# A list schedule gets a new cost of a matmul, a longer step on one engine, and a port shared by VectorE and GpSimd

## The chip, the cores and the metric

The kernel runs on one core of one Trainium2 chip. The metric is the device time of one execution in microseconds (us), lower is better. Engines are named as in the profile: PE is TensorE (matmuls), PEld its weight loads, DVE is VectorE, ACT is ScalarE, POOL is GpSimd, and SP issues the DMAs.

## The reference

A decoder trunk of two layers over 256 tokens of 2048 features, all float32. Layer 0 mixes the tokens by an RWKV-7 recurrence, layer 1 by a gated DeltaNet; behind each stands a gated MLP whose up projection goes through a causal convolution of width 3. After each of the four sub-layers the sum with the residual is normalised. Cut to what matters:

```python
for i in range(2):
    mix = rwkv7_time_mix(x, ...) if i == 0 else gated_deltanet(x, ...)
    x = layer_norm(ALPHA * x + mix, ...)
    h = causal_dwconv(x @ w_up, conv_w) + conv_b          # 2048 -> 2 * 5504
    gate, up = split(h)
    x = layer_norm(ALPHA * x + (silu(gate) * up) @ w_down, ...)
```

The weights are some 500 MB of float32 that are read once. The two recurrences are computed in chunks of 128 tokens; each chunk needs the inverse of a triangular matrix per head.

## The kernel before

**Products.** A float32 product is made of three f32r ones: each operand is split into hi and lo. `weights` (line 633 on) loads a weight tile `raw` of 128x1024, rounds it to `whi` on ACT, and takes `wlo = raw - whi` by `two`. A block of a projection is then a matmul of `whi` with hi and lo of the tokens side by side (512 columns) and one of `wlo` with hi alone (256 columns). The projections with tokens on the partitions (`proj_tm`, tile `tm`) use 512 columns throughout.

**Stages.** First the RWKV layer: token mixing and projections (`mixhl`), then eight units of the recurrence (`rwkv_unit`, four heads each, up to four units at a time) beside further projections; then the MLP (`ffn`: up projection, convolution on DVE in tile `acc`, `hhl` as its split result, down projection); then the DeltaNet's input projection with its convolution (tile `acc` again) beside eight more units (`gdn_unit`, up to two at a time) and its output projection; then the second MLP and the output.

**The order of the work is made by a planner.** The kernel doesn't issue instructions as they are written. `Plan.record` (line 305) takes each down with its estimated cost from `cost` (line 578), and with the instructions that it depends on. Consecutive matmuls into one tile are one step of at most 700 ns. There is one main stream (the projections) and one side stream per unit of a recurrence. `order` (line 366) is a list schedule: it keeps for each engine the time at which it is free, and again and again issues the candidate with the earliest start. On PE a side stream goes ahead of the main one at the same start; on the other engines the older unit goes first and the main stream last. A step is ready when what it depends on has ended, plus a latency: `LAT` and `LAT_TO` between engines, nothing from PE to PE, and `LAT_SAME` = 60 ns on one and the same other engine. The order found is static: every engine then runs its own list in turn and waits by semaphores, and the DMAs that SP issues stand in that order too.

**The choice of the engine is the planner's.** `two` (line 302) takes down an element-wise operation of two tensors with two forms, on DVE and on POOL, and `copy` one on ACT and on DVE. The candidate of a form sorts by its start plus what the form costs above the cheaper one, so the engine that ends first gets it. Estimated are, for n elements of a partition, n / 0.96 + 68 ns on DVE (1135 at 1024, 601 at 512, 335 at 256) and 2.1 n + 150 on POOL (2300, 1225, 688). The start of such a step may lie before steps that are already issued on other engines, since its place in the sorting is later than its start.

**What is not in the plan.** Each engine's steps are taken to last their estimate whatever the others do. Of the matmul, `cost` says max(107, n / 2.4 + 3) ns at full clock (216 at 512 columns, 110 at 256), doubled for float32 operands; the plan also models PE's clock, full or half, by how busy PE was.

Of the kernel before, what the change touches and what calls it, by code (L numbers as in the profile page):

```python
# [12 lines left out]
F32 = mybir.dt.float32  # L13
F32R = mybir.dt.float32r
U32 = mybir.dt.uint32
AF = mybir.ActivationFunctionType
ALU = mybir.AluOpType
AX = mybir.AxisListType

P = 128  # L20
T = 256
D = 2048
KB = D // P
# [8 lines left out]
# columns of the parameter array  # L32
# [9 lines left out]
# columns of the constant array  # L42
# [8 lines left out]
def constants():  # L51
# [10 lines left out]
    # inside a block of 32 the blocks of 8; inside a block of 8 the diagonal  # L62
    parts["blk8"] = i[:, None] // 8 % 4 == i[None, :32] // 8
    parts["eye8"] = i[:, None] % 8 == i[None, :8]
    # -1 where row and column lie in the same block of 32 but the row's block of 8 comes after the column's;
    # rows and columns in the order of digits (block of 8 in its block of 32, block of 32, place in 8)
    parts["neg32"] = -parts["blk32"][:, :96]
    o = digits()
# [10 lines left out]
def digits():  # L79
    """The tokens of a chunk ordered by block of 8 in its block of 32, then by block of 32."""  # L80
    return np.arange(P).reshape(-1, 4, 8).transpose(1, 0, 2).ravel()


class Buf:
    """A tile of a pool; it comes to be when the first instruction that touches it is issued."""
# [39 lines left out]
def arranged(x, pat, kw):  # L125
    """rearrange for numpy."""
# [27 lines left out]
class View:  # L154
    """A part of a Buf, as the instructions take it."""
# [25 lines left out]
    def region(self):  # L181
        """What it covers: the partitions and the elements of a partition, as bits. A bank of PSUM goes as one."""
# [53 lines left out]
class Op:  # L236
    __slots__ = ("lazy", "eng", "calls", "dur", "preds", "succ", "soft", "at", "bufs", "news", "stream", "idx", "npred", "ready",
                 "out", "fn", "alts", "least", "held", "evac", "table")
# [15 lines left out]
class Plan:  # L254
    """Takes instructions down in the order of the program, then issues them in an order in which the engines,
    each of which runs its instructions in turn, wait little for each other: a list schedule by estimated costs.
    The hazards between them fix what may change places; Tile draws the waits for the order issued."""
# [10 lines left out]
    # ---------------------------------------------------------------- taking down  # L268
# [7 lines left out]
    def op(self, eng, stream):  # L276
# [3 lines left out]
        o.npred, o.held, o.evac, o.lazy, o.table = 0, 0.0, [], self.lazy, None  # L280
        stream.ops.append(o)
# [11 lines left out]
    def either(self, *forms):  # L293
        """Forms (engine, function, arguments, keywords) of one instruction: the engine that ends first gets it."""
        o = self.record(*forms[0], also=[v for f in forms[1:] for v in parts(*f[2:])[1]])
        o.alts = {eng: (fn, a, kw, cost(eng, fn, a, kw, parts(a, kw)[1])) for eng, fn, a, kw in forms}
        o.least = min(x[3] for x in o.alts.values())

# [6 lines left out]
    def record(self, eng, fn, args, kw, also=()):  # L305
# [11 lines left out]
        o.dur += dur  # L317
        if fn == "activation":
            o.table = TABLES.get(args[2])
# [1532 lines left out]
```

## Time and profile before

| | |
|---|---|
| median of 3 runs | 3161.74 us (3155.25 to 3171.25) |
| the profiled execution, from its first to its last instruction | 3153.7 us |
| PE busy in it | 3008.4 us (95%) |
| DVE busy | 2374.1 us (75%) |
| ACT busy | 1688.0 us (54%) |
| POOL busy | 748.4 us (24%) |
| mean granted clock of PE | 0.982 of full |
| HBM read | 498 MB, 159 GB/s over the span |

No time is given of the profiled execution beside its span. Busy time is the union of an engine's instructions; PE's ends are modelled, so that a PE shown as 100% busy still says nothing about the pace of its matmuls, which follows from their number in a stretch. Every instruction is recorded by one helper (line 558), so groups are told apart by the names of their tiles: `wlo<-raw,whi` is the instruction that writes `wlo` from `raw` and `whi`.

### The profile page before, as it was taken

The numbers are of one execution on the slowest core, as the hardware profiler recorded it, in microseconds if no ns is written. First come the engines' busy times: TensorE is split into PE (matmuls) and PEld (weight loads), VectorE is DVE, ScalarE is ACT, GpSimd is POOL, SyncE is SP. The second block draws the span as 40 slices with busy tenths as digits, with TensorE's granted clock in tenths as the row PEclk, the third lists the DMA queues.
The fourth block names the chain that finished last, engine by engine and source line by source line (L and its number), as shares of the span: only waits on it lengthen the run. The fifth ranks groups of instructions, "written<-read, shape, count | busy, mean of one in ns | idle before, by whom it ended". The sixth has DMA issues, their size and how long they took to land.

```text
span 3153.7 us, 47051 instructions
## 1 busy us (share of the span) xinstructions
PE 3008.4 (95%) x17379; PEld 2569.3 (81%) x17379; DVE 2374.1 (75%) x3817; ACT 1688.0 (54%) x2895; POOL 748.4 (24%) x666
## 2 busy tenths in 40 slices
PE   8898988899999999999899999999999999999998
PEld 6786777788888888888788888888788888888886
DVE  6878888877877776446989989889777877777445
ACT  4555555545555555334555555556556555555333
POOL 2524345523310100002322221223133401010001
PEclk9998999999999999999999999999999999999999
DMA  6453112125666665554645555454455666565555
GB/s 207 149 164 105 62 53 77 67 94 177 193 188 188 188 188 189 191 187 157 191 136 145 154 153 148 134 147 142 146 179 171 204 190 187 187 187 184 194 189 188
DMA packets 436230, 503.19 MB, mean 160 GB/s; under 512 B 22784, under 2 KB 367264, under 8 KB 436000
## 3 DMA queue, kind: packets, MB, share of 16 engines
q1 hardware_dynamic: 436000, 500.19, 50.3%
q8 instruction: 136, 2.23, 0.3%
q14 instruction: 94, 0.77, 0.1%
HBM read 498.00 MB, written 2.13 MB: 159 GB/s over the span
## 4 chain that ended last, share of the span: by engine, by line
PE 74%; DVE 16%; issue 4%; ACT 3%; POOL 2%; DMA 1%; SPq 0%; DVEq 0%; ACTq 0%; POOLq 0%
PE mm L558 44%; PE tm L558 22%; DVE wlo L558 4%; DVE acc L558 2%; DVE mixt L558 1%; PE y L558 1%; ACT whi L558 1%; PE gm L558 1%; PE au L558 1%; DVE y L558 1%; PE n L558 1%; DVE c L558 1%; DVE uc L558 1%; PE kv L558 1%; DVE glo L558 0%
## 5 line engine op out<-in xcount | busy, mean ns | idle before, releaser
L558 PE MATMUL mm<-xhl,whi 128*128 128x512 f32 (+1 forms) x4376 | 1525.4, 395 | 4.4 <-POOL xhl L558 2.2
L558 DVE TENSOR_TENSOR wlo<-raw,whi 128x1024 fp32r<-128x1024 f32 (+2 forms) x894 | 1105.3, 1238 | 538.1 <-ACT whi L558 535.5
L558 ACT CAST whi<-raw 128x1024 fp32r<-128x1024 f32 (+3 forms) x929 | 949.4, 1023 | 748.6 <-PE tm L558 291.9
L558 PE MATMUL mm<-xhl,wlo 128*128 128x256 f32 (+1 forms) x4376 | 1209.4, 281 | 12.2 <-DVE wlo L558 11.4
L558 PEld LDWEIGHTS mm<-xhl,whi 128*128 128x128 f32 x4376 | 816.6, 189 | 177.8 <-POOL xhl L558 3.3
L558 PEld LDWEIGHTS mm<-xhl,wlo 128*128 128x128 f32 x4376 | 825.7, 189 | 29.9 <-DVE wlo L558 15.3
L558 PE MATMUL tm<-whi,hhl 128*128 128x512 f32 x1312 | 408.1, 392 | 0.0
L558 PE MATMUL mm<-mixhl,whi 128*128 128x512 f32 (+1 forms) x832 | 313.7, 414 | 13.4 <-DVE mixhl L558 8.1
L558 DVE SCALAR_TENSOR_TENSOR acc<-pre,taps,acc 128x256 f32<-128x256 f32 x536 | 312.1, 590 | 7.1 <-ACT acc L558 0.3
L558 PEld LDWEIGHTS tm<-whi,hhl 128*128 128x128 f32 x1312 | 246.4, 188 | 54.7
L558 POOL TENSOR_TENSOR hhl<-acc,hhl 128x256 fp32r<-128x256 f32 x86 | 96.4, 1121 | 814.3 <-ACT hhl L558 814.3
L558 PE MATMUL mm<-mixhl,wlo 128*128 128x256 f32 (+1 forms) x832 | 245.1, 300 | 16.3 <-DVE wlo L558 13.6
L558 PE MATMUL tm<-wlo,hhl 128*128 128x512 f32 x656 | 256.7, 391 | 0.7 <-DVE wlo L558 0.6
L558 ACT COPY addp<-mm 128x256 f32<-128x256 f32 x321 | 118.0, 368 | 175.1 <-PE mm L558 174.8
L558 PEld LDWEIGHTS mm<-mixhl,whi 128*128 128x128 f32 (+1 forms) x832 | 162.3, 197 | 50.6 <-DVE mixhl L558 8.4
L558 PEld LDWEIGHTS mm<-mixhl,wlo 128*128 128x128 f32 (+1 forms) x832 | 164.1, 197 | 28.5 <-DVE wlo L558 18.7
L558 POOL TENSOR_TENSOR wlo<-raw,whi 128x1024 fp32r<-128x1024 f32 (+3 forms) x35 | 72.6, 2078 | 406.4 <-ACT whi L558 395.1
L558 PE MATMUL tm<-whi,ohl 128*128 128x512 f32 x480 | 156.6, 398 | 0.2 <-DVE zt L558 0.2
L558 ACT ACTIVATE acc<-pre,taps 128x256 f32<-128x256 f32 x236 | 135.7, 575 | 24.0 <-DVE pre L558 23.5
L558 PEld LDWEIGHTS tm<-wlo,hhl 128*128 128x128 f32 x656 | 123.2, 188 | 27.6 <-DVE wlo L558 1.5
L558 DVE TENSOR_TENSOR pre<-mm,addp 128x256 f32<-128x256 f32 x236 | 99.0, 419 | 56.8 <-ACT addp L558 56.2
L558 POOL TENSOR_TENSOR mixhl<-mixt,mixhl 128x256 fp32r<-128x256 f32 x71 | 78.4, 1125 | 138.5 <-ACT mixhl L558 138.5
(346 smaller groups left out, 3644.0 us busy)
## 6 DMA issues: line engine op xcount, KB each, us to landing
raw<-in_ffn_w_up SPq DMA_DIRECT2D x336, 512.0 KB, 3.6
raw<-in_gdn_w_in SPq DMA_DIRECT2D x192, 512.0 KB, 3.8
raw<-in_ffn_w_down SPq DMA_DIRECT2D x168, 512.0 KB, 3.6
raw<-in_gdn_w_out SPq DMA_DIRECT2D x64, 512.0 KB, 3.6
raw<-in_rw_w_v SPq DMA_DIRECT2D x32, 512.0 KB, 3.3
raw<-in_rw_w_r SPq DMA_DIRECT2D x32, 512.0 KB, 3.3
raw<-in_rw_w_o SPq DMA_DIRECT2D x32, 512.0 KB, 3.6
raw<-in_rw_w_k SPq DMA_DIRECT2D x31, 512.0 KB, 4.4
```

The source lines that it names most:

```text
L558: i = getattr(getattr(self.real, o.eng), fn)(*(val(a) for a in args), **{k: val(a) for k, a in kw.items()})
```

## The change

Nothing that is computed changes, and no instruction is added or removed; the planner's model changes, and with it the order of the steps and which of DVE, POOL and ACT gets a step with several forms. The cost of a matmul becomes max(111, n / 2.4 + 3 + 16 n / 512) ns (232 at 512 columns, 118 at 256; the floor of float32 ones 2 x 111). `LAT_SAME` becomes 115. And steps of DVE and POOL may be marked as users of a shared port; one that would start within the last marked step of the other engine starts at that one's end.

```diff
     def either(self, *forms):
+        o.port = {eng: ported(eng, fn, a, parts(a, kw)[1]) for eng, fn, a, kw in forms}
     def record(...):
+        o.port[eng] = ported(eng, fn, args, rds)
     def order(self):
+        port = {e: (0.0, 0.0) for e in PORT}
...
                         if b.read is not None and b.read[0] != e:
                             r = max(r, b.read[1] + LAT[b.read[0]] + LAT_TO[e])
+                    if e in PORT and o.port[e]:
+                        t0, t1 = port[PORT[e]]
+                        if t0 <= max(f, r) < t1:
+                            r = t1
                     s = max(f, r)
                     if o.alts:
                         s += o.alts[e][3] - o.least
...
             t = s + dur
+            if e in PORT and o.port[e]:
+                port[e] = s, t
+PORT = {"vector": "gpsimd", "gpsimd": "vector"}
+def ported(eng, fn, args, rds):
+    if eng == "gpsimd":
+        return bool(rds)
+    if eng != "vector":
+        return False
+    wide = [v for v in rds if math.prod(v.shape[1:]) > 1 and not (v.buf.pool is not None and v.buf.pool.psum)]
+    out = args[0].buf.pool
+    return len(wide) > 1 or bool(wide) and fn in ("tensor_copy", "tensor_scalar") and not (out is not None and out.psum)
 def cost(eng, fn, args, kw, rds):
-            return 2 * max(107.0 * out.shape[0] / P, n / 1.2 + 3)
-        return max(60.0 if fn == "transpose" and args[1].dtype == F32R else 107.0 * out.shape[0] / P, n / 2.4 + 3)
+            return 2 * max(111.0 * out.shape[0] / P, n / 1.2 + 3)
+        return max(111.0 * out.shape[0] / P, n / 2.4 + 3 + 16 * n / 512)
-LAT_SAME = 60.0
+LAT_SAME = 115.0
```

So marked are: on POOL whatever reads a tensor; on DVE an operation with two or more tensors from SBUF, and a copy or `tensor_scalar` from SBUF to SBUF. The rest of the diff takes comments out.

## Rows read from the trace of the kernel before

**Rows 1.** Busy time by stretch; columns as in the first line.

```profile
core 0: us, PE busy (x) PEld busy (x) DVE busy (x) ACT busy (x) POOL busy (x), PEclk, DMA share, GB/s
0.00:900.00 900.00, 816.07 (x5144) 695.03 (x5145) 717.05 (x1239) 483.32 (x962) 354.63 (x352) 0.95 0.39 125
230.00:690.00 460.00, 407.07 (x2909) 348.25 (x2908) 383.58 (x777) 248.70 (x570) 212.02 (x220) 0.92 0.22 74
1000.00:1100.00 100.00, 100.00 (x572) 87.12 (x571) 72.08 (x100) 58.18 (x90) 11.20 (x10) 1.00 0.61 188
1400.00:2500.00 1100.00, 1050.97 (x6265) 901.25 (x6264) 924.33 (x1647) 614.95 (x1098) 295.45 (x233) 0.99 0.52 157
1500.00:2300.00 800.00, 759.49 (x4782) 655.93 (x4780) 704.09 (x1318) 447.08 (x805) 186.69 (x131) 0.99 0.51 150
2500.00:3154.00 654.00, 641.51 (x3342) 546.18 (x3341) 415.01 (x525) 328.61 (x466) 59.16 (x48) 0.99 0.58 189
```

**Rows 2.** PE's waits over the whole span: us in total, times, longest.

```profile
PE mm L558 <- DVE wlo L558: 25.0, 20, 3.3
PE blocks L558 <- DVE spread L558: 16.6, 9, 4.3
PE gm L558 <- DVE glo L558: 9.6, 4, 4.4
```

**Rows 3.** Timeline from 405 to 420 us: start, us, engine, instruction, [idle before].

```profile
409.45 5.66 POOL L558 TENSOR_TENSOR wlo<-raw,whi 128x1024 fp32r<-128x1024 f32 x2
...
410.04 2.87 DVE L558 TENSOR_TENSOR ld<-lt,cst 128x512 fp32r<-128x512 f32 x1
412.83 2.35 DVE L558 TENSOR_TENSOR t<-blocks,v 128x56 f32<-128x56 f32 x1
...
416.71 0.68 DVE L558 TENSOR_TENSOR glo<-AR,ghi 128x512 fp32r<-128x512 f32 x1
...
417.44 0.58 PE L558 MATMUL gm<-glo,ghi 64*128 64x256 f32 x2 [4.42 <-DVE glo L558]
...
417.86 0.41 DVE L558 TENSOR_TENSOR_SCAN c<-one,sw_u 128x128 f32<-128x128 f32 x1
```

**Rows 4.** DVE's groups by shape, 1500 to 2300 us: busy us, mean ns | idle before.

```profile
L558 DVE TENSOR_TENSOR wlo<-raw,whi 128x1024 fp32r<-128x1024 f32 x210 | 265.4, 1264 | 37.8 <-ACT whi L558 35.9 <-ACT th L558 0.2
L558 DVE SCALAR_TENSOR_TENSOR acc<-pre,taps,acc 128x256 f32<-128x256 f32 x192 | 113.4, 611 | 1.1 <-ACT acc L558 0.3
...
L558 DVE SCALAR_TENSOR_TENSOR z_u<-th,zt 128x256 f32<-128x256 f32 x32 | 20.3, 635 | 0.3 <-ACT th L558 0.2
...
L558 DVE SCALAR_TENSOR_TENSOR v_u<-th,acc 128x256 f32<-128x256 f32 x32 | 13.2, 417 | 0.1
```

**Rows 5.** DVE's groups by shape, 900 to 1300 us (up projection).

```profile
L558 DVE TENSOR_TENSOR wlo<-raw,whi 128x1024 fp32r<-128x1024 f32 x137 | 167.8, 1225 | 102.8 <-ACT whi L558 102.8
L558 DVE SCALAR_TENSOR_TENSOR acc<-pre,taps,acc 128x256 f32<-128x256 f32 x124 | 66.3, 535 | 2.1
```

**Rows 6.** DVE's groups by shape, 230 to 690 us (RWKV units).

```profile
L558 DVE TENSOR_TENSOR wlo<-raw,whi 128x1024 fp32r<-128x1024 f32 x39 | 51.3, 1318 | 10.3 <-ACT whi L558 10.2
L558 DVE TENSOR_TENSOR_SCAN c<-one,sw_u 128x128 f32<-128x128 f32 x32 | 20.5, 672 | 0.0
```

**Rows 7.** Timeline of DVE from 1003 us: two dependent steps, then the next.

```profile
1003.86 0.99 DVE L558 SCALAR_TENSOR_TENSOR acc<-pre,taps,acc 128x256 f32<-128x256 f32 x2
1004.89 0.42 DVE L558 TENSOR_TENSOR acc<-acc,gs 128x256 f32<-128x256 f32 x1
```

**Rows 8.** PE's main matmuls of 512 columns, 1500 to 2300 us.

```profile
L558 PE MATMUL mm<-xhl,whi 128*128 128x512 f32 x1504 | 537.1, 398 | 0.0
```

**Rows 9.** POOL's groups by shape: `hhl` over the span, `ld` and `y` in 1500 to 2300 us.

```profile
L558 POOL TENSOR_TENSOR hhl<-acc,hhl 128x256 fp32r<-128x256 f32 x86 | 96.4, 1121 | 814.3 <-ACT hhl L558 814.3
...
L558 POOL TENSOR_TENSOR ld<-lt,cst 128x512 fp32r<-128x512 f32 x16 | 24.4, 1544 | 0.0
...
L558 POOL TENSOR_TENSOR y<-z,cst 128x512 fp32r<-128x512 f32 x15 | 21.0, 1404 | 88.7 <-ACT z L558 68.3 <-DVE z L558 20.2
```

More of the change, by code (lines that the diff above doesn't have):

```diff
@@ L237 @@
     __slots__ = ("lazy", "eng", "calls", "dur", "preds", "succ", "soft", "at", "bufs", "news", "stream", "idx", "npred", "ready",
-                 "out", "fn", "alts", "least", "held", "evac", "table")
+                 "out", "fn", "alts", "least", "held", "evac", "table", "port")
 class Stream:
@@ L280, in op @@
         o.npred, o.held, o.evac, o.lazy, o.table = 0, 0.0, [], self.lazy, None
+        o.port = {}
         stream.ops.append(o)
```

## The prediction, made before the changed kernel was run

> **What bounds the kernel now.** I first read the busy time by stretch. In the up projection every microsecond of PE is taken, at full clock [rows 1]; there a stretch of 100 us holds 572 matmuls, 286 pairs of 512 and 256 columns, so a pair takes 349.7 ns. No order of the steps can make these stretches shorter. What an order can win is PE's idle time elsewhere: 900 - 816.07 = 83.9 us up to 900 us, 1100 - 1050.97 = 49.0 us from 1400 to 2500 us, and 12.5 us in the last stretch. Inside these lie the two stages of the recurrences, with 52.9 us idle of 460 (230 to 690 us) and 40.5 of 800 (1500 to 2300 us); DVE is busy for 83% and 88% of them, so it has 76.4 and 95.9 us idle [rows 1]. In the first of them the granted clock is 0.92, in the second 0.99.
>
> The second view is that of PE's waits: the longest totals are all ended by DVE (`wlo` 25.0 us, `spread` 16.6, `glo` 9.6) [rows 2]. So PE is the bound, and where it stalls it stalls for a DVE that is behind its plan.
>
> The third view says why it is behind. In the timeline POOL runs two `wlo` from 409.45 us for 5.66 us; the DVE steps `ld` and `t` that overlap them take 2.87 and 2.35 us, while `glo`, as large as `ld`, takes 0.68 us when POOL is quiet, and PE waits 4.42 us for DVE [rows 3]. The reader is to see that two engines which share nothing in the old plan hold each other up.
>
> **The change part by part.** No instruction comes or goes; the plan's order and the choice between DVE, POOL and ACT do. I price four parts.
>
> *The port.* What the collisions take from DVE has no row of its own, so I bound it by groups of one shape. From 1500 to 2300 us: 210 `wlo` at 1264 ns against 1225 in the up projection lose 8.2 us; 192 `acc` at 611 against 535 lose 14.6; 32 `z_u` at 635 against 417 of `v_u`, of the same shape, lose 7.0 [rows 4, 5]. That is 29.8 of the 399 us that these groups are busy, 7.5%, or 53 us of DVE's 704. From 230 to 690 us: 39 `wlo` at 1318 lose 3.6 us of 51.3 (7%), and 32 scans `c` at 672 against 410 in the timeline lose 8.4 of 20.5 (41%) [rows 3, 5, 6]; the two together lose 17%, or 64 of DVE's 384 us, with 27 and 157 as ends. In sum some 117 us of locked DVE time in the two stages.
>
> How much of it will the new test avoid? It moves a start only if that falls inside the other engine's *last* marked step. Two kinds are shown. `hhl` becomes ready in the middle of a DVE `wlo`, and POOL took all 86 at 1121 ns each [rows 9]; that kind is caught, since POOL must now wait for the same instant at which DVE is free. The two `wlo` on POOL [rows 3] were put there because DVE had a backlog; such a step is planned with a start that lies before DVE's last step, so the test passes it by, though DVE's next marked steps then wait for it in the plan as well. Between nothing and all I take half, one kind of the two: 58 us. Of that the end sees what PE no longer waits for: at least PE's share of the two engines' idle time, 93 / (93 + 172) = 0.35, at most all of it. I take a half, near the low end because DVE has idle time to absorb the rest: **-29 us**.
>
> *Steps that go from POOL to DVE.* In the up projection DVE is 72% busy beside a full PE, so 86 `hhl` at some 0.42 us cost nothing; were DVE full there, they would cost 36 us. In the DeltaNet units the 31 `ld` and `y` [rows 9] would bring DVE at most 31 x 0.68 = 21 us, against 96 us idle, and come out 0.8 us earlier each, 25 us in all on chains. I set the two against each other: **0**, ends -25 and +21.
>
> *The longer step on one engine.* Two dependent `acc` and the start of the next step stand 515 ns apart (1004.89 - 1003.86, halved) [rows 7]; the plan's cost of one is 396, so the real gap is 119 ns, which 115 meets and 60 does not. In 1500 to 2300 us the 192 `acc` make at most 128 such gaps, 15 us of DVE that other steps can now be planned into; by the same share of 0.35, less what was filled anyway: **-3 us**, ends -15 and 0.
>
> *The pace of the matmuls.* The row gives 349.7 ns a pair [rows 1]; the old cost is 326, the new one 350. So the plan had PE 24 ns a pair too fast, and with 1504 pairs [rows 8] PE came to its places in the DeltaNet stage up to 36 us later than planned. That error was a cushion: DVE could be late without PE waiting. It goes. If half the port (26 us) and the gaps (15 us) are now planned instead, 41 us of planned lateness stand in for 36 us of cushion, and little is lost; I put **+3 us**, ends 0 and +36.
>
> The Trainium skill, "TensorE: Matmul & The Clock Gate", section "Back-to-back issue gap", speaks against this part: it gives N / 2.4 + 2.5 ns from matmul to matmul, 325 ns a pair, by which the old cost was right and the new one too slow. By it the new plan would place side work where PE stands 36 us too early, and the sum would be some 30 us higher, no gain at all. The measured 349.7 ns decides against the page here, so the sum goes by the row and this way gets no chance of its own.
>
> SP's loads move with the steps that free their buffers. The DMA share is 0.22 to 0.61 in these stretches [rows 1] and no wait of PE's above is ended by a DMA, so I price that at nothing; a load on the path would cost PE what it waits for it.
>
> The sum: -29 + 0 - 3 + 3 = -29 us on the profiled execution, 3153.7 - 29 = 3124.7. That execution lies 8.0 us under the median of the runs, so I forecast 3124.7 + 8.0 = **3133 us**, 0.9% less.
>
> **The rivals.** *The chains stay (within 0.5%).* DVE loses less to the port, but what it wins is its own idle time: a unit's next step still waits for a matmul, and PE stalls at the same places for the same chains. For it: DVE has 172 us idle in the two stages while PE waits for it. Against: in rows 3 the wait is the collision itself. Priced with a tenth avoided, seen by PE at the low end: 117 x 0.1 x 0.35 = 4 us, so 3158, and 16 us either way of the median counts as the same.
>
> *The cushion is missed (slower).* Place: the DeltaNet stage, where 1504 pairs stand beside an 88% busy DVE. Mechanism: side matmuls are now put into PE's fixed list 24 ns a pair earlier, while backlogged POOL steps escape the test, so DVE is as late as before and PE waits for it. Price: 36 us less the 15 us of gaps now planned, +21, so 3183 us. It decides if under a third or so of the locked time is avoided. For it: the escape is in the code. Against: most of what collides in rows 4 is an in-order neighbour of a `wlo`, the kind the test sees.
>
> *The change does not bite.* The test passes nearly all by and the greedy order comes out much as before: 3162 us, within the run-to-run spread of 3155 to 3171. For it: DVE is saturated enough for starts in the past to be common. Against: two costs change beside it, and every tie after the first is drawn anew.
>
> **How the numbers follow.** A measurement of this kernel tells about 0.5%, 16 us, from no change. Forecast 0.46 (faster), chains 0.26 and no bite 0.06 (within), cushion 0.22 (slower). The low end is three quarters of the locked time avoided and three quarters of that seen by PE, 117 x 0.56 = 66 us: 3095. The high end is the cushion's 3183 and a little for the runs: 3185. A lower bound than this would need the clock as well: 0.92 over 460 us leaves up to 37 us in the RWKV stage if PE, less often idle, were granted full clock throughout, which I do not count. The forecast's own range is 3095 to 3146.
>
> **What would show it.** Right: the group `hhl` moves largely to DVE; `acc` and `z_u` from 1500 to 2300 us come down towards 535 and 417 ns; PE's waits on `wlo`, `spread` and `glo` shrink; PE's idle time in the two stages falls from 93 us to some 65; 100 us of up projection still hold 572 matmuls. Wrong: the DVE groups get shorter and PE's idle time doesn't (chains); PE's idle time from 1500 us on rises past 60 us with waits ended by DVE (cushion); POOL keeps its groups and their mean times (no bite). A change of the time in the MLP stretches would contradict all of it.

## The result, and the profile after

The changed kernel takes **3217.11 us** (median of 4 runs, 3203.66 to 3220.57); the kernel before, run beside it, 3163.12 us (4 runs, 3155.25 to 3171.25). The ratio is **1.0143, 95% interval 1.0113 to 1.0173**: slower by 1.4%, where 0.9% less was forecast, and outside the range.

The profiled executions have spans of 3153.7 us (before) and 3202.0 us (after). I cut both at the same marks of the program: the first product of an RWKV unit, the first product of the first MLP's up projection, its down projection, the DeltaNet projections, the DeltaNet output projection, and the second MLP. The first view is the busy time by stretch. For the kernel before, its RWKV units with the projections that run beside them, then the MLP's up projection:

```profile
core 0: us, PE busy (x) PEld busy (x) DVE busy (x) ACT busy (x) POOL busy (x), PEclk, DMA share, GB/s
250.40:742.30 491.90, 440.94 (x3060) 376.05 (x3059) 405.21 (x812) 261.18 (x583) 218.71 (x226) 0.93 0.24 79
742.30:1236.70 494.40, 489.06 (x2817) 425.92 (x2816) 364.61 (x507) 288.29 (x459) 82.94 (x74) 1.00 0.61 186
1475.10:2209.50 734.40, 692.52 (x4443) 601.80 (x4442) 656.56 (x1255) 416.77 (x768) 190.12 (x136) 0.99 0.52 149
2209.50:2411.60 202.10, 199.63 (x981) 164.46 (x979) 150.74 (x230) 112.61 (x196) 55.61 (x53) 0.99 0.47 165
```

The last two lines are its DeltaNet units and the DeltaNet output projection. The same stretches of the changed kernel follow, with 100 us of its up projection and the 800 us that answer to the last stretch but one of [rows 1]:

```profile
247.50:777.20 529.70, 473.83 (x3060) 406.18 (x3059) 411.01 (x796) 262.50 (x591) 232.72 (x234) 0.85 0.22 73
777.20:1276.10 498.90, 491.90 (x2818) 428.75 (x2817) 357.42 (x531) 289.38 (x460) 73.15 (x50) 0.99 0.60 184
...
1000.00:1100.00 100.00, 100.00 (x572) 87.07 (x571) 69.57 (x103) 57.91 (x90) 9.76 (x5) 1.00 0.60 188
...
1514.80:2254.20 739.40, 696.52 (x4467) 605.93 (x4466) 648.68 (x1252) 420.34 (x775) 179.25 (x127) 0.98 0.51 147
2254.20:2455.00 200.80, 195.16 (x957) 160.51 (x955) 157.63 (x258) 111.13 (x192) 36.81 (x35) 1.00 0.48 168
...
1540.00:2340.00 800.00, 753.83 (x4752) 651.31 (x4750) 695.84 (x1324) 442.93 (x794) 186.50 (x124) 0.98 0.50 148
```

37.8 of the 48.3 us that the span grew lie in the RWKV stage, and it isn't waiting that grew there. PE's idle time in it is 491.9 - 440.94 = 51.0 us before and 529.7 - 473.83 = 55.9 us after. What grew is its *busy* time: as many matmuls, 3060, take 32.9 us longer, and the granted clock is 0.85 where it was 0.93. By (1 - clock) x length, what TensorE lacks to its full clock in this stage went from 34 us to 79. Over the whole span, with the clocks that the two profiles show (0.982 and 0.965), it went from 57 to 112, 55 us more in a span that is 48.3 longer. The up projections give 4.5 us (494.4 to 498.9) and about as much in the second MLP; the DeltaNet units 5 (734.4 to 739.4), in which PE is idle for 42.9 us where it was 41.9.

Where the clock is lost, a finer cut of the changed kernel shows, and under it the same view for the projections' matmuls alone (those that read `mixhl`; the output projection's, which read `yhl`, begin later, at 569 us before and at 607 us after):

```profile
500.00:520.00 20.00, 18.88 (x145) 16.52 (x144) 14.65 (x27) 11.15 (x28) 13.79 (x17) 1.00 0.08 27
520.00:540.00 20.00, 8.51 (x38) 6.29 (x38) 18.34 (x43) 8.74 (x22) 10.16 (x12) 0.58 0.12 40
540.00:560.00 20.00, 19.75 (x122) 17.04 (x120) 8.68 (x18) 9.72 (x27) 1.97 (x5) 0.50 0.00 1
560.00:580.00 20.00, 20.00 (x87) 18.52 (x88) 7.06 (x22) 4.25 (x12) 7.37 (x8) 0.50 0.17 53
580.00:600.00 20.00, 19.19 (x120) 17.36 (x119) 17.12 (x37) 8.13 (x17) 7.88 (x7) 0.71 0.37 111
...
520.00:560.00 40.00, 0.84 (x2) 0.55 (x2) 0.00 (x0) 0.00 (x0) 0.00 (x0) 0.54 0.06 20
560.00:600.00 40.00, 13.11 (x45) 9.27 (x46) 0.00 (x0) 0.00 (x0) 0.00 (x0) 0.61 0.27 82
```

From 520 us PE is busy for 8.51 us of 20, and the granted clock falls from 1.00 to 0.50, which is 1.2 GHz. Then PE is busy all the time, and the clock stays at 0.50 for 40 us more: what it works on are the units' small products, beside 2 matmuls of the projections from 520 to 560 us. It rises as the projections come back. In the kernel before, 520 to 560 us hold 62 of them at a clock of 0.88:

```profile
480.00:520.00 40.00, 12.58 (x52) 9.15 (x53) 0.00 (x0) 0.00 (x0) 0.00 (x0) 0.93 0.16 53
520.00:560.00 40.00, 17.67 (x62) 11.78 (x61) 0.00 (x0) 0.00 (x0) 0.00 (x0) 0.88 0.33 113
```

What the half clock costs one instruction shows in PE's groups by shape, first in 541 to 579 us, then in 600 to 638 us of the changed kernel (busy us, mean ns):

```profile
L569 PE MATMUL au<-u,lt 128*128 128x64 f32 x16 | 3.8, 417 | 0.0
L569 PE MATMUL mm<-mixhl,whi 128*128 128x512 f32 x5 | 3.3, 657 | 0.0
...
L569 PE MATMUL mm<-mixhl,whi 128*128 128x512 f32 x10 | 3.6, 393 | 0.0
L569 PE MATMUL au<-u,lt 128*128 128x64 f32 x16 | 2.1, 276 | 0.0
```

Then what the change was to do. The groups that answer to [rows 4] (DVE, 1540 to 2340 us), [rows 6] (DVE, 247.5 to 777.2 us) and [rows 9] (POOL):

```profile
L569 DVE TENSOR_TENSOR wlo<-raw,whi 128x1024 fp32r<-128x1024 f32 x210 | 274.3, 1306 | 33.5 <-ACT whi L569 32.4
L569 DVE SCALAR_TENSOR_TENSOR acc<-pre,taps,acc 128x256 f32<-128x256 f32 x188 | 100.9, 564 | 2.4 <-ACT acc L569 1.7
L569 DVE SCALAR_TENSOR_TENSOR z_u<-th,zt 128x256 f32<-128x256 f32 x32 | 16.7, 531 | 0.0
...
L569 DVE TENSOR_TENSOR wlo<-raw,whi 128x1024 fp32r<-128x1024 f32 x42 | 52.5, 1251 | 14.9 <-ACT whi L569 13.8 <-PE lora L569 0.8
L569 DVE TENSOR_TENSOR_SCAN c<-one,sw_u 128x128 f32<-128x128 f32 x32 | 17.4, 563 | 0.0
...
L569 POOL TENSOR_TENSOR hhl<-acc,hhl 128x256 fp32r<-128x256 f32 x42 | 79.9, 1903 | 806.1 <-ACT hhl L569 806.1
```

Half of the `hhl` left POOL, and the rest take 1903 ns instead of 1121. `acc`, `z_u` and `c` came down a part of the way (611 to 564, 635 to 531, 672 to 563), but `wlo` went up in 1540 to 2340 us, from 1264 to 1306. DVE's busy time there fell by 8 us (704.09 to 695.84), and in the RWKV stage it rose by 6 with 16 steps fewer. PE's waits that answer to [rows 2], over the whole span:

```profile
PE blocks L569 <- DVE spread L569: 26.9, 8, 8.1
PE mm L569 <- DVE wlo L569: 24.8, 17, 3.3
PE mm L569 <- DVE mixhl L569: 9.8, 2, 9.6
...
PE gm L569 <- DVE glo L569: 3.9, 2, 3.2
```

`wlo` is as it was, `spread` is longer by 10 us, and the waits for `glo` fell from 9.6 us to 3.9; the wait of 8.1 us is the one at 520 us, just ahead of the stretch at half clock.

### The profile page after: what moved, and what is told of

It reads as the page before. It is cut to its first block, busy times and chain, and to the rows that moved or that the text cites. A ratio compares the mean times of both kernels' runs of the same rounds, so it can differ in the third digit from the quotient of the medians.

```text
span 3202.0 us, 47006 instructions
## 1 busy us (share of the span) xinstructions
PE 3044.8 (95%) x17379; PEld 2604.6 (81%) x17379; DVE 2374.7 (74%) x3884; ACT 1692.9 (53%) x2906; POOL 695.0 (22%) x588
## 4 chain that ended last, share of the span: by engine, by line
PE 68%; DVE 9%; issue 3%; ACT 2%; POOL 2%; DMA 1%; DVEq 0%; POOLq 0%; ACTq 0%
PE mm L569 39%; PE tm L569 22%; DVE wlo L569 3%; DVE acc L569 1%; PE y L569 1%; ACT whi L569 1%; PE au L569 1%; PE n L569 1%; PE gm L569 0%; PE kv L569 0%; DVE uc L569 0%; PE yT L569 0%; PE o L569 0%; PE u L569 0%; PE du L569 0%
## 5 line engine op out<-in xcount | busy, mean ns | idle before, releaser
L569 DVE TENSOR_TENSOR wlo<-raw,whi 128x1024 fp32r<-128x1024 f32 (+1 forms) x900 | 1109.1, 1234 | 546.4 <-ACT whi L569 543.4
L569 DVE SCALAR_TENSOR_TENSOR acc<-pre,taps,acc 128x256 f32<-128x256 f32 x536 | 277.4, 541 | 6.7 <-ACT acc L569 1.7
L569 POOL TENSOR_TENSOR hhl<-acc,hhl 128x256 fp32r<-128x256 f32 x42 | 79.9, 1903 | 806.1 <-ACT hhl L569 806.1
L569 POOL TENSOR_TENSOR wt<-raw,wt 128x512 fp32r<-128x512 f32 x9 | 12.7, 1413 | 451.5 <-ACT wt L569 451.5
L569 PEld LDWEIGHTS tm<-whi,ohl 128*128 128x128 f32 x480 | 90.2, 188 | 21.2 <-DVE zt L569 1.8
```

Of the source, the lines that this page charges most:

```text
L569: i = getattr(getattr(self.real, o.eng), fn)(*(val(a) for a in args), **{k: val(a) for k, a in kw.items()})
```

## The experiments

The theories that the runs were to tell apart: **the port rule** (P in the expectations) spoils the RWKV stage; **the cushion** (C) of the old matmul cost is missed (the rival of the prediction); **scatter** (S), a greedy schedule whose order any edit of its costs redraws; and **starved projections** (H), in which the order leaves a stretch of the RWKV stage to the units' products, and TensorE falls to half clock. Ratios are to the kernel before, run beside each (medians of 3163 to 3170 us). "The loss" is (1 - granted clock) x length of the RWKV stage, with the clock as the view prints it, to two places.

### The parts, one at a time

The kernel before with the new matmul cost alone:

```
-            return 2 * max(107.0 * out.shape[0] / P, n / 1.2 + 3)
-        return max(60.0 if fn == "transpose" and args[1].dtype == F32R else 107.0 * out.shape[0] / P, n / 2.4 + 3)
+            return 2 * max(111.0 * out.shape[0] / P, n / 1.2 + 3)
+        return max(111.0 * out.shape[0] / P, n / 2.4 + 3 + 16 * n / 512)
```

> Only the matmul cost is the new one (111 and 16 n / 512); the port is not looked at and LAT_SAME is 60. Theory P (the port part spoils the RWKV stage): the time stays within 10 us of before, PE's first matmul of the first MLP (mm<-xhl) starts at 742 us give or take 8, and no stretch at half clock is longer than 15 us. Theory C (the lost cushion of 24 ns a pair): 15 to 40 us over before, with PE's idle time from 1500 to 2300 us (40.5 before) up by 10 us or more. Theory S (scatter: any other order of the greedy list lands somewhere else in the RWKV stage): the first mm<-xhl moves by 5 to 35 us either way, all of the time's difference lies before it, and the DeltaNet stage keeps its length within 6 us.

Measured 3220.2 us, ratio 1.0162 (1.0127 to 1.0197), over what any of the three forecast. Its DeltaNet units and their output projection:

```profile
1514.70:2264.30 749.60, 700.56 (x4467) 606.23 (x4466) 649.71 (x1264) 420.22 (x771) 175.38 (x120) 0.98 0.52 145
2264.30:2471.20 206.90, 198.61 (x955) 162.60 (x954) 152.05 (x239) 109.62 (x189) 62.05 (x56) 0.98 0.49 164
```

Its profiled execution has a span of 3213.8 us, 60.1 more than before. Of these 38.9 lie in the RWKV stage (491.9 to 530.8) and 20.0 in the two stretches shown, where PE is idle for 57.3 us instead of 44.4: so C's sign, idle time up by 10 us or more, is there too, at the smaller part of the loss. The kernel before with LAT_SAME alone:

```
-LAT_SAME = 60.0
+LAT_SAME = 115.0
```

> Only LAT_SAME is the new one (115). Theory P: within 10 us of before. Theory C: within 10 us of before, or a few us faster, as the cushion is kept and DVE's steps are planned better. Theory S: off by 5 to 35 us either way in the RWKV stage, the rest of the time unchanged within 8 us.

Measured 3156.98 us, 0.9961 (0.9942 to 0.9979): the only kernel of the study below the kernel before beyond its interval. Where the 13 us come from the profiles don't show: the execution profiled here took 3159.45 us, the one of the kernel before 3155.25. The port rule alone (`ported`, `port` and the test in the loop over candidates, with the old costs):

```
+                    if e in PORT and o.port[e]:
+                        t0, t1 = port[PORT[e]]
+                        if t0 <= max(f, r) < t1:
+                            r = t1
```

> Only the port is new; matmul cost and LAT_SAME are the old ones. Theory P: 30 to 50 us over before, the first mm<-xhl at 770 us or later, with a stretch at half clock of 30 us or more between 450 and 650 us. Theory C: 10 to 40 us faster than before, since the cushion is kept and DVE is locked less. Theory S: off by 5 to 35 us either way, all of it in the RWKV stage.

Measured 3183.14 us, 1.0045 (1.0024 to 1.0066): 13 us over before, not P's 30 to 50, and within the range of S. Then the changed kernel with one part taken out, first the matmul cost, then the port test:

```
-            return 2 * max(111.0 * out.shape[0] / P, n / 1.2 + 3)
-        return max(111.0 * out.shape[0] / P, n / 2.4 + 3 + 16 * n / 512)
+            return 2 * max(107.0 * out.shape[0] / P, n / 1.2 + 3)
+        return max(60.0 if fn == "transpose" and args[1].dtype == F32R else 107.0 * out.shape[0] / P, n / 2.4 + 3)
```

> The changed kernel with the old matmul cost: port and LAT_SAME 115 stay. Theory C (the new pace is what costs, by the lost cushion): at or under before, 3140 to 3165 us, with a DeltaNet stage of 725 us or less. Theory H (what costs is a stretch of the RWKV stage in which the main projections have next to nothing ready, so that PE falls to half clock): this order too has such a stretch, so the RWKV stage is 20 to 40 us longer than before's 491.8, with over 55 us lost to half clock in it, whatever the cost of a matmul; in all 3165 to 3195.

```
-                    if e in PORT and o.port[e]:
+                    if False and o.port[e]:
```

> The changed kernel without the port: the new pace and LAT_SAME 115. Theory C: slower still than the changed kernel, as the cushion is gone and nothing stands for it: 3215 us or more. Theory H: the RWKV stage is again some 450 us plus what half clock loses in it, 510 to 535 us, and the total 3190 to 3225.

Measured 3236.43 us, 1.0216 (1.0177 to 1.0255) without the matmul cost, and 3226.64 us, 1.0194 (1.015 to 1.0237) without the port rule. The first missed both its forecasts. Its RWKV stage is starved (553.2 us, a loss of 89), as H had it, and its DeltaNet units are short (703.8 us), as C had it, but the output projection behind them took 251.2 us instead of 202.1. The second came out as C forecast (3215 or more) and just over H's range. Taking either part out makes the changed kernel no faster. The port rule and LAT_SAME cost +0.45% and -0.4% alone and +2.2% together, so the parts have no prices that add up. The cushion doesn't explain the changed kernel: with the old matmul cost back it is the slowest of all, and PE's idle time in its DeltaNet units, where the cushion would be missed, rose by 1 us only. Nor is the port rule the one cause, since without it the kernel is as slow.

### An edit that means nothing

The kernel before with LAT_SAME moved by 2 ns, up and then down:

```
-LAT_SAME = 60.0
+LAT_SAME = 62.0
```

> The kernel before with LAT_SAME 62 in place of 60: a change of the model by 2 ns that means nothing. Theories P and C: within 6 us of before, since nothing of port or cushion changes. Theory S: 8 us or more off before, either way, in the RWKV stage, though the model is the same to 2 ns.

```
-LAT_SAME = 60.0
+LAT_SAME = 58.0
```

> The kernel before with LAT_SAME 58 instead of 60, an edit that says nothing of the hardware. Its order has a stretch poor in the projections' wide matmuls near the middle of the RWKV stage and one at its end. Starved projections: 3170-3190, loss by the clock in the stage over 45 us. Without that theory: as the kernel before, 3155-3175.

Measured 3186.89 us, 1.0065 (1.0043 to 1.0087) for 62, which S alone allowed, and **3215.3 us, 1.0157 (1.0131 to 1.0183)** for 58: an edit of 2 ns that tells the planner nothing new costs as much as the whole change. It missed what was expected on the upper side. Its RWKV stage and, in it, the projections' matmuls:

```profile
249.10:786.90 537.80, 478.89 (x3059) 411.72 (x3058) 406.76 (x815) 260.71 (x582) 212.16 (x224) 0.84 0.22 72
...
480.00:520.00 40.00, 15.29 (x64) 11.19 (x64) 0.00 (x0) 0.00 (x0) 0.00 (x0) 0.91 0.13 40
520.00:560.00 40.00, 0.00 (x0) 0.00 (x0) 0.00 (x0) 0.00 (x0) 0.00 (x0) 0.52 0.06 20
560.00:600.00 40.00, 14.45 (x64) 10.27 (x64) 0.00 (x0) 0.00 (x0) 0.00 (x0) 0.80 0.37 119
```

It is the changed kernel's picture: 40 us without one matmul of the projections, a clock of 0.52 there, 0.84 over the stage, and the same matmuls busy for 478.89 us instead of 440.94. A neighbour of the changed kernel:

```
-LAT_SAME = 115.0
+LAT_SAME = 117.0
```

> The changed kernel with LAT_SAME 117 instead of 115, an edit without meaning. Its order has the same poor stretch in the middle of the RWKV stage, and a milder one behind it. Starved projections: 3190-3212, loss 55-75 us. Scatter without a cause: 3160-3240. If it and another neighbour stay above 3190 the slowdown belongs to the new rules and not to one unlucky order.

Measured 3215.62 us, 1.0166 (1.0131 to 1.0201), with a stage of 535.4 us at 0.84: as slow as the changed kernel, and slower than expected. Here 2 ns moved the time by no more than the noise. By what was put on record, two neighbours over 3190 would lay the slowdown on the new rules; the kernel before at LAT_SAME 58, which has none of them and is as slow, speaks against that reading.

### One slot more for what starves

A projection's output waits in one of eight slots (`uin`) until its unit has used it; when all are held, no projection can end, and none of its matmuls can go beside the units. That is read from the code; no trace shows that the slots are what is missing at 520 us of the changed kernel. A ninth slot, paid for with one of the units' work slots, in the changed kernel and in the kernel before:

```
-DEPTH_R, NS2_R, NIN, NC8_R = 4, 27, 8, 5
+DEPTH_R, NS2_R, NIN, NC8_R = 4, 26, 9, 5
```

> The changed kernel with all three parts, and nine slots in place of eight for what the projections hand to a unit (NIN 9), paid by one working slot of the units (NS2_R 26 in place of 27). Theory H: the main projections can run ahead of the units again, the long stretch at half clock goes (none over 25 us), the RWKV stage comes back to 480 to 505 us, and the total to 3160 to 3185, though the model is the changed one. Theory C: the DeltaNet stage and the cushion are untouched, so at most 10 us come back: 3205 or more.

> The kernel before with the same edit as the first run with nine slots (NIN 9, NS2_R 26). Starved projections: the kernel before has no long starved stretch to cure and pays one work slot: 3160-3190. If a ninth slot is worth 20 us to any order: 3140-3150.

Measured 3196.46 us, 1.0094 (1.0059 to 1.0129) for the changed kernel, and 3193.98 us, 1.0094 (1.0061 to 1.0127) for the kernel before. The same edit takes 21 us off the one and puts 27 on the other, and both missed what H expected: the stages are 520.1 us (480 to 505 expected) and 538.0. The ninth slot paid for in other groups, in the changed kernel:

```
-DEPTH_R, NS2_R, NIN, NC8_R = 4, 27, 8, 5
+DEPTH_R, NS2_R, NIN, NC8_R = 4, 27, 9, 4
...
-NMORE, NLNT = 8, 4
+NMORE, NLNT = 8, 3
```

> The changed kernel with nine slots instead of eight for what the projections hand to the units, paid for in two other groups (NC8_R 4, NLNT 3) and not in the units' work slots as in the run with nine before. Starved projections: in this order the projections' wide matmuls stand evenly between the units' products through the whole stage, so the RWKV stage is at most 510 us, the loss by the granted clock there at most 50 us, and the time 3160-3185. Mere scatter of the greedy schedule: no preference, 3195-3235 as for the other orders under the new costs.

Measured 3191.74 us, 1.0083 (1.0053 to 1.0113). Its RWKV stage came out as expected (and a loss of 51 us against at most 50). The stage, its projections' matmuls (those that read `mixhl`) in 520 to 560 us, and the DeltaNet units:

```profile
248.70:755.30 506.60, 449.71 (x3059) 382.37 (x3058) 416.67 (x802) 260.02 (x589) 232.71 (x229) 0.90 0.24 77
...
520.00:560.00 40.00, 11.86 (x54) 7.95 (x53) 0.00 (x0) 0.00 (x0) 0.00 (x0) 0.91 0.34 106
...
1494.70:2238.30 743.60, 700.39 (x4468) 609.60 (x4467) 650.45 (x1252) 421.10 (x776) 180.07 (x124) 0.97 0.52 146
```

506.6 us at 0.90, 23 less than in the changed kernel, with the port rule and both costs in place. The time missed its 3160 to 3185, since the rest of the loss isn't in this stage: the DeltaNet units took 743.6 us, and each up projection some 7 more than before. So an order under the new rules need not have the starved stretch, and without it about half of the 48 us is gone. That the slot is the reason is not shown, since the edit redraws the order as any other does.

### The port rule without its escape

The prediction held that the test passes many collisions by, since it looks at the other engine's last step alone. This kernel, the port rule alone with the old costs, looks at the last 64 and at the whole length of the step:

```
+        port = {e: deque(maxlen=64) for e in PORT}
...
+                        n = o.alts[e][3] if o.alts else o.dur
+                        for t0, t1 in port[PORT[e]]:
+                            if t0 < max(f, r) + n and max(f, r) < t1:
+                                r = t1
```

> The port alone, but so that a marked step never overlaps any of the last 64 marked steps of the other engine: the escape is closed. If locked time is what the end sees (the reason of the prediction): DVE's collisions fall to a few us, and the time is under before by 15 us or more. Theory H: POOL loses most of its two-tensor steps to DVE, the units' chains get longer, the main projections starve and PE's clock falls: 3230 us or more, with the collisions gone.

Measured 3179.34 us, 1.004 (1.0023 to 1.0057), between the two forecasts. The RWKV stage, the DeltaNet units and the DeltaNet output projection, and two of DVE's groups in 1510 to 2200 us:

```profile
231.80:768.40 536.60, 503.47 (x3068) 432.12 (x3067) 375.17 (x851) 268.15 (x608) 117.77 (x162) 0.81 0.23 73
...
1498.10:2170.10 672.00, 661.22 (x4251) 581.97 (x4249) 592.59 (x1195) 407.40 (x748) 86.52 (x65) 0.99 0.57 161
2170.10:2433.70 263.60, 234.36 (x1172) 194.12 (x1171) 189.78 (x363) 131.45 (x240) 21.85 (x26) 0.90 0.39 129
...
L570 DVE SCALAR_TENSOR_TENSOR acc<-pre,taps,acc 128x256 f32<-128x256 f32 x192 | 90.7, 496 | 0.9 <-ACT acc L570 0.5
L570 DVE SCALAR_TENSOR_TENSOR z_u<-th,zt 128x256 f32<-128x256 f32 x32 | 13.8, 443 | 0.0
```

Here the collisions are gone or nearly so: `acc` takes 496 ns and `z_u` 443, against 611 and 635 in [rows 4]. PE is idle for 33.1 us in the RWKV stage (51.0 before) and 10.8 in the DeltaNet units (41.9). And no time is won. In the RWKV stage PE's matmuls take 503.47 us at a clock of 0.81. (In this order the units begin 18.6 us earlier, so the stage ends 26 us later than before, though it is 45 us longer.) In the DeltaNet part the units end 62 us earlier, but fewer of the main matmuls have gone beside them: the output projection behind them takes 263.6 us with 1172 matmuls instead of 202.1 with 981, 29 of them idle, at a clock of 0.90, and the two together 935.6 against 936.5.

### Does the clock cost that time, and can it be bought?

One answer needs no new kernel. Executions of one kernel run the same instructions in the same order, and yet differ in the granted clock. Of 25 executions of the kernel before, timed beside the first experiments, the one of 3153.22 us had a clock of 0.983 and the one of 3181.01 us 0.973. By (1 - clock) x span they lack 54 and 86 us, 32 more for a time that is 28 longer; over the 72 executions beside the experiments time and clock go together (correlation -0.93). So lost clock comes out as time, about one for one, with the order held fixed; what makes the clock differ between executions the record doesn't show.

To move the clock on purpose, I left the order of a kernel as it is and put extra matmuls of 384 columns ahead of unit products that open a bank of PSUM, where the plan has few columns of matmul. They are overwritten by the product behind them:

```
+                n = min(4, math.ceil(max(0.0, FILL * SLICE - wide[k]) / 160.0 / left[k]))
...
+                for _ in range(n):
+                    self.real.tensor.matmul(news(o)[0].get()[:, :384], p[:, :P], p, start=True, stop=True)
```

In the changed kernel (FILL 0.5, then 0.7), in the full port rule (0.6), and in the kernel before with LAT_SAME 115 (0.7):

> The changed kernel, its order untouched, with 128 extra matmuls (384 columns, into a bank that the next real product overwrites) put between the unit products of the RWKV stage where the order has few wide ones. They add work and take none away: worked out by their columns, about 20 us at the full clock, 40 at half. If the stage is long because TensorE stands at half clock where only the units' small products run (80 us lost of 529.6, by the granted clock), the loss falls under 50 us and the time to 3175-3200. If the half clock only accompanies an order that is longer for other reasons, the extra work is paid in full: 3230-3260.

> The same with 308 extra matmuls (about 49 us of work at the full clock). Clock theory: the loss by the granted clock falls under 35 us, and the time to 3165-3205, since part of the extra work lies where TensorE would stand idle or at half clock. Rival: 3255-3310.

> The kernel with the full port rule alone (VectorE's and GpSimd's port steps never beside each other; 3179.3 us, TensorE idle in the two recurrence stages 44 us against 93 before, but 104 us lost to the half clock in the RWKV stage), with 347 extra matmuls in the RWKV stage. Clock theory: the port rule's gain comes to light once the clock stays up: loss under 60 us, 3120-3160, below the kernel before. Rival (the half clock costs nothing by itself): 3215-3260.

> The kernel before with LAT_SAME 115 alone (3157.0 us; 46 us lost to the half clock in the RWKV stage) with 122 extra matmuls there, about 20 us of work at the full clock. Clock theory: the loss falls to 20-30 us, the time to 3135-3155. Rival: 3170-3190.

Measured 3212.98 us, 1.0138 (1.0096 to 1.0181); 3232.93 us, 1.0201 (1.0164 to 1.0238); 3164.85 us, 0.9991 (0.9967 to 1.0015); 3170.77 us, 1.0006 (0.9986 to 1.0026). None reached the clock theory's time, and none but the last the rival's; of the losses (66, 50, 32 and 31 us) only the third came out as low as expected. The traces have 137, 327, 363 and 153 extra matmuls. The stage of the full port rule with them, then in it the extra matmuls by themselves and the kernel's own instructions by themselves:

```profile
230.90:769.30 538.40, 515.58 (x3431) 439.30 (x3430) 375.62 (x851) 268.43 (x608) 120.97 (x162) 0.94 0.23 73
...
230.90:769.30 538.40, 101.82 (x363) 64.67 (x363) 0.94 0.23 73
...
230.90:769.30 538.40, 448.54 (x3068) 382.06 (x3067) 375.62 (x851) 268.43 (x608) 120.97 (x162) 0.94 0.23 73
```

The clock rose from 0.81 to 0.94, and the kernel's own products cover 448.54 us instead of 503.47, at least 55 us less, in the same order and on the same data. (Own and extra matmuls overlap in the trace, so the two rows can't be taken from each other; the loss by the clock fell by 70 us, from 102 to 32.) So the half clock has a price here. The 102 us of extra work did not make the kernel slower: by the medians it is 14 us faster than without them (3179.34 to 3164.85, and the intervals of the two ratios lie apart). The stage shown, 538.4 us against 536.6, hides that, since it is of an execution of 3178.82 us, the longest of its ten. Elsewhere the bargain was worse. In the changed kernel 45 us of extra work changed the time by -4 us, which is noise, and 95 us by +16; in the kernel with LAT_SAME 115, whose loss was small, 52 us cost 14. In all four the time rose by far less than the work put in. Part of that work fell into PE's idle time (17 us in the second kernel), but the clock rose in all four, so wide matmuls do buy clock; but only where most clock was missing did that pay, and none came below the kernel before beyond its interval. The rest has to come from the order.

### Two orders chosen by their evenness

Last, two orders picked only by how evenly the projections' matmuls stand between the units' products: an even one with the port rule, and an uneven one without any new rule.

The port rule alone:

```
-LAT_SAME = 60.0
+LAT_SAME = 90.0
```

> The port rule alone with LAT_SAME 90, chosen of some orders because the projections' matmuls stand in it evenly between the units' products through the whole RWKV stage. Starved projections: RWKV stage 490-505 us, loss by the clock 30-50 us, time 3145-3170. An order's evenness tells nothing: 3155-3220, as the orders tried so far.

The kernel before:

```
-LAT_SAME = 60.0
+LAT_SAME = 130.0
```

> The kernel before with LAT_SAME 130, chosen because its order has a long stretch with few of the projections' matmuls late in the RWKV stage and a shorter one early, though no cost in it differs for the port or the matmul's pace. Starved projections: loss over 75 us, RWKV stage over 525, time 3190-3230. An order's evenness tells nothing: 3155-3220, as likely below 3185 as above.

Measured 3194.4 us, 1.0094 (1.0065 to 1.0122), and 3202.99 us, 1.0125 (1.0098 to 1.0152). The uneven one came as forecast: a stage of 540.1 us at a clock of 0.84, 48 us longer than in the kernel before, with none of the new rules. The even one has the shorter stage of the two by 31 us, 509.5 at 0.89, though not the 490 to 505 expected, and its time missed, while the rival's 3155 to 3220 holds both times. Clock was lost again later, this time with PE idle as well, in the DeltaNet output projection, of which the second line is the worst part:

```profile
2204.10:2450.30 246.20, 223.54 (x1115) 184.44 (x1113) 177.56 (x310) 122.50 (x216) 42.41 (x39) 0.92 0.41 136
2300.00:2350.00 50.00, 30.15 (x139) 25.19 (x138) 21.60 (x38) 13.47 (x30) 5.71 (x4) 0.61 0.11 35
```

With the units ahead of it, which were shorter (713.7 us), that part took 959.9 us instead of 936.5. So evenness in one stage bears on the length of that stage, and doesn't settle the time of the kernel.

### All RWKV stages side by side

Length, PE's busy time and matmuls, and granted clock, each from the row of that kernel's stage in the busy time by stretch; the loss is (1 - clock) x length. Each row is one profiled execution; that of the kernel before is one of its shorter ones (3155.25 us, where the medians beside the runs are 3163 to 3170), so a difference of 15 us or so between two rows tells nothing. The ratios are of medians.

| kernel | ratio | stage us | PE busy (x) | clock | loss us |
|---|---|---|---|---|---|
| before | 1 | 491.9 | 440.94 (3060) | 0.93 | 34 |
| LAT_SAME 115 alone | 0.9961 | 493.5 | 444.94 (3060) | 0.91 | 44 |
| changed, ninth slot from other groups | 1.0083 | 506.6 | 449.71 (3059) | 0.90 | 51 |
| port rule, LAT_SAME 90 | 1.0094 | 509.5 | 454.20 (3074) | 0.89 | 56 |
| before, LAT_SAME 62 | 1.0065 | 513.0 | 463.98 (3059) | 0.88 | 62 |
| changed, ninth slot for a work slot | 1.0094 | 520.1 | 463.02 (3059) | 0.89 | 57 |
| port rule alone | 1.0045 | 526.8 | 470.47 (3073) | 0.88 | 63 |
| **changed** | **1.0143** | **529.7** | **473.83 (3060)** | **0.85** | **79** |
| matmul cost alone | 1.0162 | 530.8 | 483.35 (3060) | 0.84 | 85 |
| changed, LAT_SAME 117 | 1.0166 | 535.4 | 479.50 (3059) | 0.84 | 86 |
| full port rule alone | 1.004 | 536.6 | 503.47 (3068) | 0.81 | 102 |
| before, LAT_SAME 58 | 1.0157 | 537.8 | 478.89 (3059) | 0.84 | 86 |
| before, ninth slot for a work slot | 1.0094 | 538.0 | 486.53 (3059) | 0.84 | 86 |
| before, LAT_SAME 130 | 1.0125 | 540.1 | 484.84 (3059) | 0.84 | 86 |
| changed without the port rule | 1.0194 | 543.6 | 483.77 (3061) | 0.84 | 87 |
| changed without the matmul cost | 1.0216 | 553.2 | 487.73 (3074) | 0.84 | 89 |

Length less loss is 446 to 465 us in every line but that of the full port rule (435), where PE waits least; the loss runs from 34 to 102. The stage's length goes with the clock, whatever was edited. The kernel's time does so less well, since orders differ in the later stages too. And of the fifteen other orders fourteen are slower than the kernel before beyond their intervals: its own order is a good draw, and to redraw it cost 1.1% on the mean of the fifteen; how its constants were chosen is not on record.

## Why the prediction was wrong, point by point

**What bounds the kernel** was read right for the MLPs: a stretch of 100 us (1000 to 1100) still holds 572 matmuls, and the up projections changed by 4.5 us, of which 2.6 are two longer waits of PE for `wlo`. For the recurrences it was read too narrowly. The prediction said that what an order can win is PE's idle time. An order also sets how fast PE's *busy* time goes by, and that is where most of the 37.8 us went: PE was busy for 32.9 us more, idle for 4.9 more.

**The port, first factor (half of 117 us of locked time avoided): failed.** The reading of [rows 3] and the size of the lock hold, as the full rule shows: without collisions `z_u` takes 443 ns of its 635, and DVE's busy time falls by 30 us in the RWKV stage and 64 in the DeltaNet units, there with 60 steps fewer. (`acc` came down to 496 ns there, so the 535 that the prediction took as free of collisions was not quite free.) But the test of the change gave back 8 us of DVE in 800 us of the DeltaNet stage, and in the RWKV stage DVE was busy for 6 us more. Priced as the prediction priced it, the groups of [rows 4] lost 26 us after and 29.8 before: an eighth was avoided there, not half. Those of [rows 6] lost 6 us and 12, half, and it did not show in DVE's total. That the escape is what took the rest fits the full rule, which closes it. `hhl` was the kind that the prediction called caught: half stayed on POOL, and by their 1903 ns collide harder than before.

**The port, second factor (half of it seen by the end): failed.** PE's idle time in the two stages was to fall from 93 us to some 65. It is 98.8 (55.9 and 42.9), 6 us more, so of the -29 us nothing came. Nor does more of the port bring it: with the escape closed PE is idle for 49 us less in the two stages, and the time is 0.4% longer. PE's saved idle time came back as half clock in the RWKV stage (loss 34 to 102 us) and as idle time and half clock in the output projection.

**Steps from POOL to DVE** (0, from -25 to +21): the DeltaNet units as a whole moved by 5 us, the up projections by 4.5 each, which fits the term; no run isolates it.

**LAT_SAME** (-3, from -15 to 0) lies inside its ends when alone, at 13 us less by the medians. That the gap of 119 ns is the reason isn't shown: 58, 62 and 130 are all slower than 60, so the time doesn't follow the constant.

**The matmul cost** (+3, from 0 to +36) was misplaced. Alone it costs 50 us by the medians, over its upper end. Of the 60 us between the profiled executions 20 lie in the DeltaNet units and their output projection, near the 21 to 36 at which the prediction priced the cushion without the port rule; 39 lie in the RWKV stage, for which it had no term. One order can't tell whether the 20 are the cushion or the draw. In the changed kernel these two stretches grew by 3.7 us (936.5 to 940.2), as the +3 said. So the rival with the right sign, at 0.22, had the wrong place and mechanism: PE's idle time in the DeltaNet units hardly rose, and putting the old cost back makes the changed kernel slower. On the cost itself the pairs of [rows 1] stand: 572 matmuls in 100 us.

**The clock** is the step that decides: a term that the sum put at nothing. It stands in the prediction as a gain of up to 37 us that it didn't count, and nowhere as a cost. By (1 - clock) x length it cost 45 us in the RWKV stage (34, then 79), where the span grew by 48.3. The same product could be made with the other sign: 0.92 over 460 us was already a loss, and a redrawn order could double it, as it did. The plan does carry PE's clock, but only as a longer step: the next candidate is chosen by the earliest start, and nothing in that choice avoids a stretch of small products.

**The chances** left out a case. Every number above prices what the rules say; none the redrawing itself. LAT_SAME 58, 62 and 130 in the kernel before, with nothing to tell the planner about the port or the matmul, gave 1.0157, 1.0065 and 1.0125, and fourteen of fifteen other orders are slower. Against that spread the change's 1.0143 is not large.

**What stays open.** That the time went into a starved stretch at half clock is shown by the trace, and that half clock costs time in a fixed order, by the executions at different clocks and by the extra matmuls. Why the projections have nothing to issue there is read from the code and not shown. That the *new rules* make such stretches likelier is not shown. The six kernels with the new matmul cost all lie between 1.0083 and 1.0194; those with the old one between 0.9961 and 1.0216. Both kinds have starved orders, and too few were run to tell their means apart. Nor was the other half of the 48 us settled, which the ninth slot from other groups did not bring back. No version but LAT_SAME 115 alone (0.4%) beat the kernel before beyond its interval.

## What to carry to other kernels

Ahead of pricing an edit of a scheduler's costs, run two or three edits of it that mean nothing: their spread is what any rule has to beat, and the prices of its parts won't add up below it. Here 2 ns cost the kernel before 0.65 and 1.6%, and the changed kernel nothing beyond noise. In a stage where long streams of wide matmuls are mixed with small dependent ones, read the granted clock beside PE's busy time, and look for stretches in which the wide ones are missing: work moved out of PE's idle time is won only if the clock stays up. What keeps the wide ones coming may be a count of slots rather than a cost.

## What the runs showed of the hardware that was not expected

- PE can be busy for 100% of a stretch and keep the half clock: 540 to 580 us of the changed kernel, 39.7 of 40 us busy with 208 matmuls, nearly all of 256 columns or fewer, at 0.50 throughout.
- In the kernel with the full port rule 363 extra matmuls of 384 columns in one stage, 102 us of work, left the time 14 us shorter by the medians (3179.34 to 3164.85): the clock of the stage went from 0.81 to 0.94, and the kernel's own products took at least 55 us less.
- Executions of one kernel, in one order, differ in the granted clock, and the time goes with it: 0.983 and 3153.22 us, 0.973 and 3181.01 us.
- A POOL step of 128x256 can be held to 1903 ns on average where it was 1121 in another order, though there were half as many of them.
